# Linear attention gate and suffix decay sums: from float32 matmuls to stacked and split float32r matmuls

## The chip, the cores and the metric

The kernel runs on one core of a Trainium2 chip. The metric is the device time of one execution in microseconds (us). Three runs of the kernel before took 1291.74, 1292.12 and 1295.21 us (median 1292.12). One further execution was recorded by the hardware profiler, and all durations below come from it.

## The reference

One layer of a hybrid encoder is computed for a prompt of 512 tokens and for 8 samples of 16 tokens each (640 rows in all): three token mixers in parallel (stick-breaking attention, a pooling mixer, gated linear attention), cross attention, and a SwiGLU network. The change touches only the decay gates of the linear attention:

```python
log_a = log_sigmoid(lr @ w_gla_a2 + b_gla_a) / 16          # lr: rows x 16, w_gla_a2: 16 x 384
def step(S, inp):                                          # one chunk: 64 prompt rows, or 16 sample rows
    qc, kc, vc, ac = inp
    b = cumsum(ac, axis=1)
    o_inter = einsum('blhk,bhkv->blhv', qc * exp(b), S)
    decay = exp(where(causal, b[:, :, None] - b[:, None, :], -inf))
    att = einsum('bthk,bshk,btshk->bhts', qc, kc, decay)
    o_intra = einsum('bhts,bshv->bthv', att, vc)
    S_new = exp(b[:, -1])[..., None] * S + einsum('bshk,bshv->bhkv', kc * exp(b[:, -1:] - b), vc)
    return S_new, o_inter + o_intra
```

The kernel treats the prompt in four tiles of 128 rows and the eight samples as a fifth tile. The sum `b[:, -1:] - b` is a suffix sum of the gates; it is what `pd` holds below.

## The kernel before, in words

Weights and activations of the large products are held as two float32r parts, a high part (`wh_`, `hT_h`, ...) and the remainder (`wl_`, `hT_l`, ...), and each product is three matmuls (line 114). Small products, those of the linear attention among them, are plain float32 matmuls, which the trace shows as two instructions each.

Instructions of one engine run in program order. That order isn't the order of the source: a scheduler puts the instructions of all engines in order when the program is built, by its own costs and by which buffers come free. Only a few later stages fix their order by hand.

Linear attention runs tile by tile in the order 0, 1, sample, 2, 3. `gla_prep(i)` makes the gates of a tile: transposes of q and k, then `tp_lr` (L653, TensorE) and the copy `lrT` (L656, ScalarE), the gate product `z` (L658; in the rows `z_g`), three ScalarE steps and one VectorE step that give `la` (L660 to L663), the prefix sums `pb` (L667), their copy `bT` and exponential `E`, the suffix sums `pd` (L674) and their exponential. `gla_main(i)` then goes through the levels 64, 32, 16, 8, 4, 2, 1 (the sample tile through the last four): each level makes a tile `X` from `bT` (two subtractions on VectorE, L713 and L714; one, L709, at level 1), an exponential on ScalarE (L715 or L710), multiplies it by k and q (L716, L717), and has four small products `pl` (L721) whose result is copied into `attT` under a mask (L724). The products of a level are told apart by the partitions of `pl`: 64, 96, 112, 120, 124, 126, 127 for level 64 down to level 1. `X` has two buffers. The tile `la` has one buffer, which it shares with `sq` (L782) of `gla_main`.

While this goes on, TensorE also has the projections `ps_n` (the last 190 of them between the first gate and the first level), and after them the gate and branch products `ps_g` and `ps_b` of the branches a and b, which depend on nothing of the linear attention. ScalarE and VectorE turn `ps_g` into a sigmoid (`sgm`, L816 to L819) and multiply `ps_b` by it (`mrg`), and they also split the next weights (`wh_`, L83; `wl_`, L89). Branch c needs the linear attention's output (`tp_oc`).

In the first 50 us VectorE and GpSimd build masks; the gate weights `a2` (in the trace `a`) are loaded by two transfers from GpSimd's queue. `hist` is loaded from SyncE's queue and transposed by TensorE (`tp_h`) just before the products `ps_u`.

Of the kernel before, what the change touches and what calls it, by code (L numbers as in the profile page):

```python
# [8 lines left out]
F32 = mybir.dt.float32  # L9
F32R = mybir.dt.float32r  # L10
# [3 lines left out]
ALU = mybir.AluOpType  # L14
AX = mybir.AxisListType

P = 128
# [9 lines left out]
GW = 384  # L27
# [6 lines left out]
def tile_hybrid_stream_step(  # L34
# [9 lines left out]
    nc = tc.nc  # L44
    PSUM = bass.MemoryType.PSUM

    def open_pool(name, side="left", bufs=1, **kw):
        return tc.alloc_tile_pool(name=name, bufs=bufs, side=side, reuse_waits="tile", **kw)

    const = open_pool("const")  # L50
# [12 lines left out]
    def bank(shape, tag="z", name="ps"):  # L63
        bufs = {"g": 2, "t": 2, "z": 2, "o": 2}[tag]
        return psum.tile(shape, F32, tag=tag, bufs=bufs, name=name)
# [75 lines left out]
    def split(h, l, src):  # L141

        nc.scalar.copy(h, src)  # L143
        nc.vector.tensor_tensor(l, src, h.bitcast(F32), ALU.subtract)  # L144
# [66 lines left out]
    ident = const.tile([P, P], F32, name="ident")  # L211
# [71 lines left out]
    suf = const.tile([P, P], F32, name="suf")  # L283
# [10 lines left out]
    suf_s = const.tile([P, P], F32, name="suf_s")  # L294
# [14 lines left out]
    for hh in (64, 32, 16, 8, 4, 2, 1):  # L309
# [3 lines left out]
        sel(v, [[2 * hh, nb]], hh - 1, -1)  # L313
        lmask[hh] = v
        o += nb
    a2 = const.tile([17, GW], F32, name="a2")
    nc.gpsimd.dma_start(a2[0:16, :], w_gla_a2[0])
    nc.gpsimd.dma_start(a2[16:17, :], b_gla_a[0:1, :])
    gn = const.tile([P, GW], F32, name="gn")
    nc.gpsimd.dma_start(gn, gla_norm[0:1, :].broadcast_to([P, GW]))  # L320
    psc = const.tile([P, 2], F32, name="psc")
# [6 lines left out]
    lr_nat = natc.tile([P, NT, 16], F32, name="lr_nat")  # L328
# [47 lines left out]
    for f in range(2):  # L376
        tp = bank([P, P], "t", "tp_h")
# [51 lines left out]
    for t_i in range(2):  # L429
        un = poolw.tile([P, 256], F32, tag="un", bufs=2, name="un")  # L430
        tp = bank([P, 256], "t", "tp_u")
# [25 lines left out]
    for i in range(NT):  # L457
        tp = bank([P, SBW], "t", "tp_k")
# [176 lines left out]
    glw = open_pool("glw", "right")  # L635
    S = None

    def gla_prep(i):

        sample = i == 4  # L640
        qT = glw.tile([96, 4, P], F32, tag="qT", bufs=2, name="qT")
        kT = glw.tile([96, 4, P], F32, tag="kT", bufs=2, name="kT")
        tp = bank([96, 4, P], "t", "tp_q")
        for h in range(4):
            nc.tensor.transpose(tp[:, h, :], qk_nat[:, i, h * 96:(h + 1) * 96], ident)
        nc.scalar.mul(qT, tp, 96 ** -0.5)
        tp = bank([96, 4, P], "t", "tp_k")
        for h in range(4):
            nc.tensor.transpose(tp[:, h, :], qk_nat[:, i, GW + h * 96:GW + (h + 1) * 96], ident)
        nc.scalar.copy(kT, tp)  # L650

        tp = bank([16, P], "t", "tp_lr")
        nc.tensor.transpose(tp, lr_nat[:, i, :], ident)  # L653
        lrT = glw.tile([17, P], F32, tag="lrT", name="lrT")
        nc.gpsimd.memset(lrT, 1.0)
        nc.scalar.copy(lrT[0:16, :], tp)  # L656
        z = bank([P, GW], "t", "z_g")
        nc.tensor.matmul(z, lrT, a2, start=True, stop=True)  # L658
        la = glw.tile([P, GW], F32, tag="la", name="la")
        nc.scalar.activation(la, z, AF.Abs)  # L660
        nc.scalar.activation(la, la, AF.Exp, scale=-1.0)
        nc.scalar.activation(la, la, AF.Ln, bias=1.0)
        nc.vector.scalar_tensor_tensor(la, z, 0.0, la, ALU.min, ALU.subtract)  # L663

        pb = bank([96, 4, P], "t", "pb")
        for h in range(4):
            nc.tensor.matmul(pb[:, h, :], la[:, h * 96:(h + 1) * 96], tri_s if sample else tri,  # L667
                             start=True, stop=True)
        bT = glw.tile([96, 4, P], F32, tag="bT", bufs=2, name="bT")
        nc.scalar.copy(bT, pb)  # L670
        E = glw.tile([96, 4, P], F32, tag="E", bufs=2, name="E")
        nc.scalar.activation(E, pb, AF.Exp, scale=1.0 / TAU)
        pd = bank([P, GW], "t", "pd")
        nc.tensor.matmul(pd, suf_s if sample else suf, la, start=True, stop=True)  # L674
        kd = qk_nat[:, i, 0:GW]
        nc.scalar.activation(kd, pd, AF.Exp, scale=1.0 / TAU)
        nc.vector.tensor_tensor(kd, kd, qk_nat[:, i, GW:2 * GW], ALU.mult)
        eL = glw.tile([96, 4, NB], F32, tag="eL", bufs=2, name="eL")
        if sample:
            nc.gpsimd.tensor_copy(eL, E.rearrange("p h (b t) -> p h b t", t=16)[:, :, :, 15])  # L680
        else:
            nc.gpsimd.tensor_copy(eL[:, :, 0:1], E[:, :, 127:128])
        nc.vector.tensor_tensor(E, E, qT, ALU.mult)
        return qT, kT, bT, E, eL
# [105 lines left out]

    order = (0, 1, 4, 2, 3)
    pre = gla_prep(0)
    for c in range(5, 7):
        proj_nat(c)
    for j, i in enumerate(order):
        nxt = gla_prep(order[j + 1]) if j + 1 < NT else None
        if i == 4:
            gla_main(i, pre, None)
        else:
            S = gla_main(i, pre, S)  # L800
        pre = nxt
# [34 lines left out]
    for i in range(NT):  # L836
        tp = bank([P, 3, P], "t", "tp_oc")
# [15 lines left out]
    X = resid.tile([P, NT, D], F32, name="X")  # L853
# [687 lines left out]
```

## Time and profile before

| | us |
|---|---|
| median of three runs | 1292.12 |
| profiled execution, its own time | 1288.61 |
| span from first to last instruction | 1286.9 |
| TensorE busy | 1266.3 (98%) |
| VectorE busy | 781.4 (61%) |
| ScalarE busy | 593.2 (46%) |

TensorE's share of the chain that ended last is 93%. An engine's busy time in a stretch of 40 us, subtracted from 40, is its idle time there. "Chain" below is the view of the work that ended last in a stretch, merged into pieces with start, length and count.

### The profile page before, as it was taken

To read this page: it belongs to the slowest core of one execution; us is meant where nothing else is said; L and a number is where in the kernel's file an instruction comes from. 1 tells how busy PE (TensorE), PEld (TensorE's weight loads), DVE (VectorE), ACT (ScalarE), POOL (GpSimd) and SP (SyncE) were. 2 spreads that over 40 slices of the span, in tenths; PEclk is the share of its full clock that TensorE was granted. 3 is DMA by queue.
4 is the path that set the end of the run, shared out by engine and by line. 5 is a ranking of instruction groups with operands and counts; after the bars stand their busy time and mean duration, and the time that the engine had idled before them with its cause. 6 is when DMAs were issued, how large, how long until landed. Compare 5 with 4: busy or idle time off the path is not lost.

```text
span 1286.9 us, 21366 instructions
## 1 busy us (share of the span) xinstructions
PE 1266.3 (98%) x8493; PEld 1154.1 (90%) x8493; DVE 781.4 (61%) x1465; ACT 593.2 (46%) x1191; POOL 41.3 (3%) x162
## 2 busy tenths in 40 slices
PE   8999999999999999999999999999999999999997
PEld 8998777998999999987998888889898989899996
DVE  7343876387478455537535544598466767675667
ACT  5324665455353444535444443475352525243353
POOL 2101111001000000000000000000000000000000
PEclk9999999999999999999999999999999999999999
DMA  7324332101321232232348960243132313132233
GB/s 241 100 80 118 96 102 70 47 16 56 83 65 46 83 93 75 95 131 66 118 161 301 324 228 1 82 148 94 54 107 73 99 51 113 52 99 83 83 107 123
DMA packets 132890, 133.89 MB, mean 104 GB/s; under 512 B 15798, under 2 KB 116741, under 8 KB 132789
## 3 DMA queue, kind: packets, MB, share of 16 engines
q1 hardware_dynamic: 132501, 132.23, 32.8%
q8 instruction: 67, 1.10, 0.4%
q14 instruction: 34, 0.28, 0.1%
q0 software_dynamic: 288, 0.29, 0.1%
HBM read 121.72 MB, written 10.77 MB: 103 GB/s over the span
## 4 chain that ended last, share of the span: by engine, by line
PE 93%; DVE 3%; ACT 2%; DMA 1%; issue 1%; SPq 0%; POOL 0%; DVEq 0%; ACTq 0%
PE ps_g L114 13%; PE fX L1292 11%; PE ps_d L114 8%; PE ps_n L114 7%; PE fZ L1292 5%; PE ps_xq L114 4%; PE ps_b L114 4%; PE acc L1364 4%; PE acc L1363 4%; PE acc L1365 4%; PE ps_qk L114 3%; PE fY L1292 3%; PE pl L721 2%; PE ps_xv L114 2%; PE ps_xk L114 2%; PE z L508 1%
## 5 line engine op out<-in xcount | busy, mean ns | idle before, releaser
L1363 PE MATMUL acc<-wh_o,ga_h 128*128 128x512 f32 (+1 forms) x224 | 87.3, 390 | 0.0
L1364 PE MATMUL acc<-wl_o,ga_h 128*128 128x512 f32 (+1 forms) x224 | 87.2, 389 | 0.0
L1365 PE MATMUL acc<-wh_o,ga_l 128*128 128x512 f32 (+1 forms) x224 | 87.2, 389 | 0.0
L816 ACT ACTIVATE sgm<-ps_g 128x320 f32<-128x320 f32 x48 | 20.9, 436 | 65.9 <-PE ps_g L114 65.8
L1365 PEld LDWEIGHTS acc<-wh_o,ga_l 128*128 128x128 f32 x224 | 42.0, 188 | 9.6
L1363 PEld LDWEIGHTS acc<-wh_o,ga_h 128*128 128x128 f32 x224 | 42.0, 188 | 9.3
L1364 PEld LDWEIGHTS acc<-wl_o,ga_h 128*128 128x128 f32 x224 | 42.1, 188 | 9.2
L1292 PE MATMUL fX<-fT_h,wl_f 128*128 128x320 f32 x160 | 49.5, 309 | 0.0
L1292 PE MATMUL fX<-fT_l,wh_f 128*128 128x320 f32 x160 | 49.4, 309 | 0.0
L1292 PE MATMUL fX<-fT_h,wh_f 128*128 128x320 f32 x160 | 49.4, 309 | 0.0
L1292 PE MATMUL fZ<-S_h,wl_f 128*128 128x320 f32 x160 | 49.4, 309 | 0.0
L1292 PE MATMUL fX<-S_h,wh_f 128*128 128x320 f32 x160 | 49.4, 309 | 0.0
L1292 PE MATMUL fZ<-S_l,wh_f 128*128 128x320 f32 x160 | 49.4, 309 | 0.0
L1292 PE MATMUL fX<-S_l,wh_f 128*128 128x320 f32 x160 | 49.4, 309 | 0.0
L1292 PE MATMUL fZ<-S_h,wh_f 128*128 128x320 f32 x160 | 49.4, 308 | 0.0
L1292 PE MATMUL fX<-S_h,wl_f 128*128 128x320 f32 x160 | 49.3, 308 | 0.0
L143 ACT CAST wh_f<-ra 128x1024 fp32r<-128x1024 f32 x20 | 21.0, 1051 | 45.7 <-PE acc L1365 26.8
L144 DVE TENSOR_TENSOR wl_f<-ta,wh_f 128x1024 fp32r<-128x1024 f32 x20 | 24.5, 1226 | 27.1 <-ACT wh_f L143 27.1
L817 DVE TENSOR_SCALAR sgm<-sgm 128x320 f32<-128x320 f32 x48 | 15.5, 325 | 40.4 <-ACT sgm L816 40.3
L143 ACT CAST wh_f<-ta 128x1024 fp32r<-128x1024 f32 x20 | 21.0, 1049 | 38.7 <-PE acc L1365 29.2
L144 DVE TENSOR_TENSOR wl_f<-ra,wh_f 128x1024 fp32r<-128x1024 f32 x20 | 24.4, 1222 | 22.9 <-ACT wh_f L143 22.7
L1448 DVE TENSOR_TENSOR X<-acc,X 128x512 f32<-128x512 f32 x40 | 27.2, 690 | 17.9 <-PE acc L1365 17.9
(1001 smaller groups left out, 4230.5 us busy)
## 6 DMA issues: line engine op xcount, KB each, us to landing
raw_o<-in_w_ffn_out_dram SPq DMA_DIRECT2D x22, 512.0 KB, 3.5
ra<-in_w_ffn_in_dram SPq DMA_DIRECT2D x40, 256.0 KB, 3.3
rb<-in_w_ffn_in_dram SPq DMA_DIRECT2D x40, 256.0 KB, 3.4
kc<-in_cache_mem_k_dram SPq DMA_DIRECT2D x16, 512.0 KB, 4.8
vc<-in_cache_mem_v_dram SPq DMA_DIRECT2D x16, 512.0 KB, 5.7
raw_mix<-in_w_mix_out_dram SPq DMA_DIRECT2D x8, 512.0 KB, 4.1
raw_xo<-in_w_xo_dram SPq DMA_DIRECT2D x8, 512.0 KB, 4.8
kn<-in_cache_sb_k_dram SPq DMA_DIRECT2D x24, 128.0 KB, 2.5
```

Of the source, the lines that this page charges most:

```text
L114: ins = nc.tensor.matmul(ps, a, b, start=(j == 0), stop=(j == len(todo) - 1))
L143: nc.scalar.copy(h, src)
L144: nc.vector.tensor_tensor(l, src, h.bitcast(F32), ALU.subtract)
L508: nc.tensor.matmul(z[:, j * n:(j + 1) * n], qkT[r, p_, i * P:(i + 1) * P], qkT[r, 3 + p_, 0:n], start=True, stop=True)
L721: nc.tensor.matmul(pl[0:nk, h], X[:, h, 0:nk], mv_, start=True, stop=True)
L816: nc.scalar.activation(s, ps, AF.Exp, scale=-1.0)
L817: nc.vector.tensor_scalar(s, s, 2.0 ** 63, None, ALU.min)
L1292: nc.tensor.matmul(ps, w_, m_, start=(start and j == 0), stop=(stop and j == 11), skip_group_check=True)
L1363: nc.tensor.matmul(ps, ah, wh[:, 0, c0:c0 + w], start=first, stop=False)
L1364: nc.tensor.matmul(ps, ah, wl[:, 0, c0:c0 + w], start=False, stop=False)
L1365: nc.tensor.matmul(ps, al, wh[:, 0, c0:c0 + w], start=False, stop=last)
L1448: nc.vector.tensor_tensor(dst, ps, dst, addop)
```

## The change

The gate product becomes one float32r matmul over 81 rows. The 16 columns of `lr` are split into a high and a low part and laid into columns 0 to 15 (high), 32 to 47 (low) and 64 to 79 (high) of a tile `lr3`, whose columns 16 and 80 hold ones for the bias; `a2` holds the high part of the weights in rows 0 to 16 and 32 to 47 and the low part in rows 64 to 80. The transposed tile is cast to float32r when it is copied. The suffix sums `pd` become two float32r matmuls, of the high and the low part of `la`, with the 0/1 matrix cast to float32r. The low part `la_l` takes one of the two buffers of `X`. The prefix sums `pb` stay float32.

```diff
-    a2 = const.tile([17, GW], F32, name="a2")
-    nc.gpsimd.dma_start(a2[0:16, :], w_gla_a2[0])
-    nc.gpsimd.dma_start(a2[16:17, :], b_gla_a[0:1, :])
+    a2 = const.tile([81, GW], F32R, name="a2")
+    nc.gpsimd.memset(a2.bitcast(F32), 0.0)
+    a2w = open_pool("a2w", "right")
+    a2n = a2w.tile([81, GW], F32, name="a2n")
+    for r_ in (0, 32, 64):
+        nc.gpsimd.dma_start(a2n[r_:r_ + 16, :], w_gla_a2[0])
+    for r_ in (16, 80):
+        nc.gpsimd.dma_start(a2n[r_:r_ + 1, :], b_gla_a[0:1, :])
+    a2h = a2w.tile([81, GW], F32R, name="a2h")
+    nc.vector.tensor_copy(a2[0:17, :], a2n[0:17, :])
+    nc.vector.tensor_copy(a2[32:48, :], a2n[32:48, :])
+    nc.vector.tensor_copy(a2h[64:81, :], a2n[64:81, :])
+    nc.vector.tensor_tensor(a2[64:81, :], a2n[64:81, :], a2h[64:81, :].bitcast(F32), ALU.subtract)
+    a2w.release()
+    suf_r = const.tile([P, 2, P], F32R, name="suf_r")
+    nc.vector.tensor_copy(suf_r[:, 0], suf)
+    nc.vector.tensor_copy(suf_r[:, 1], suf_s)
...
-        tp = bank([16, P], "t", "tp_lr")
-        nc.tensor.transpose(tp, lr_nat[:, i, :], ident)
-        lrT = glw.tile([17, P], F32, tag="lrT", name="lrT")
-        nc.gpsimd.memset(lrT, 1.0)
-        nc.scalar.copy(lrT[0:16, :], tp)
+        lr3 = glw.tile([P, 81], F32, tag="lr3", name="lr3")
+        lrh = glw.tile([P, 16], F32R, tag="lrh", name="lrh")
+        nc.gpsimd.memset(lr3, 0.0)
+        nc.gpsimd.memset(lr3[:, 16:17], 1.0)
+        nc.gpsimd.memset(lr3[:, 80:81], 1.0)
+        nc.scalar.copy(lrh, lr_nat[:, i, :])
+        nc.scalar.copy(lr3[:, 0:16], lrh.bitcast(F32))
+        nc.scalar.copy(lr3[:, 64:80], lrh.bitcast(F32))
+        nc.vector.tensor_tensor(lr3[:, 32:48], lr_nat[:, i, :], lrh.bitcast(F32), ALU.subtract)
+        tp = bank([81, P], "t", "tp_lr")
+        nc.tensor.transpose(tp, lr3, ident)
+        lrT = glw.tile([81, P], F32R, tag="lrT", name="lrT")
+        nc.scalar.copy(lrT, tp)
...
-        nc.tensor.matmul(pd, suf_s if sample else suf, la, start=True, stop=True)
+        la_h = glw.tile([P, GW], F32R, tag="la_h", name="la_h")
+        la_l = glw.tile([P, GW], F32R, tag="X", bufs=2, name="la_l")
+        split(la_h, la_l, la)
+        sr = suf_r[:, 1 if sample else 0]
+        nc.tensor.matmul(pd, sr, la_h, start=True, stop=False)
+        nc.tensor.matmul(pd, sr, la_l, start=False, stop=True)
```

The scheduler puts the stage of the linear attention in another order. On VectorE, this is what stands before in the first tile's levels, from the first write of `attT` (L698) on; the subtractions for level 64 and 32 were already made during the projections, far above, and the second tile's `la` stands between two subtractions of level 8:

```order
L698 TENSOR_TENSOR attT<-pa,ident 128x512
L713 TENSOR_TENSOR X<-bT 96x16x16
L724 COPY_PREDICATED attT<-lm,pl 64x4x64
L714 TENSOR_TENSOR X<-bT 96x16x16
L724 COPY_PREDICATED attT<-lm,pl 96x8x32
L713 TENSOR_TENSOR X<-bT 96x32x8
L663 SCALAR_TENSOR_TENSOR la<-z_g,la 128x384
```

With the change, at the same place, the second tile's `la` and `la_l` come first, and levels 64 and 32 of the first tile follow them:

```order
L727 TENSOR_TENSOR attT<-pa,ident 128x512
L676 TENSOR_TENSOR lr3_3156<-lr_nat_411,lrh_3157 128x16
L687 SCALAR_TENSOR_TENSOR la_2993<-z_g_2991,la_2993 128x384
L144 TENSOR_TENSOR la_l_3009<-la_2993,la_h_3008 128x384
L742 TENSOR_TENSOR X_3026<-bT_2664 96x4x64
L743 TENSOR_TENSOR X_3026<-bT_2664 96x4x64
L742 TENSOR_TENSOR X_3038<-bT_2664 96x8x32
L743 TENSOR_TENSOR X_3038<-bT_2664 96x8x32
L712 TENSOR_TENSOR E_3005<-E_3005,qT_2964 96x512
```

So all levels of a tile now stand behind the next tile's gate, in one block. On TensorE, in the second tile's last levels, this stands before between level 4 (`pl` of 124 partitions) and level 2 (126):

```order
L721 MATMUL pl<-X 124x64 x4
L114 MATMUL ps_g<-hT_l,wh_ga0b 128x320
L114 MATMUL ps_g<-hT_h,wl_ga0b 128x320
L114 MATMUL ps_g<-hT_h,wh_ga0b 128x320
L114 MATMUL ps_g<-hT_l,wh_ga0b 128x320
L114 MATMUL ps_g<-hT_h,wl_ga0b 128x320
L114 MATMUL ps_b<-oa_h,wh_ba_3847 128x320
L114 MATMUL ps_b<-oa_l,wh_ba_3847 128x320
L114 MATMUL ps_b<-oa_h,wl_ba_3849 128x320
L721 MATMUL pl<-X 126x64 x4
```

With the change, the same levels of the same tile, from level 8 (120) on:

```order
L750 MATMUL pl<-X 120x64 x4
L114 MATMUL ps_b<-oa_h,wh_ba_3929 128x320
L114 MATMUL ps_b<-oa_l,wh_ba_3929 128x320
L114 MATMUL ps_b<-oa_h,wl_ba_3931 128x320
L750 MATMUL pl<-X 124x64 x4
L750 MATMUL pl<-X 126x64 x4
L678 MATMUL tp_lr<-ident,lr_3341 81x128
L114 MATMUL ps_g<-hT_h,wh_ga1a 128x320
L114 MATMUL ps_g<-hT_l,wh_ga1a 128x320
L682 MATMUL z_g<-a_379,lrT 128x384
```

Eight large matmuls stood between level 4 and level 2; now there are none, three stand between level 8 and level 4, and two between `tp_lr` and `z_g`.

## Rows read from the trace of the kernel before

**Rows 1.** The page: span, the engines' totals, and TensorE's granted clock by slices.

```profile
span 1286.9 us, 21366 instructions
PE 1266.3 (98%) x8493; PEld 1154.1 (90%) x8493; DVE 781.4 (61%) x1465; ACT 593.2 (46%) x1191; POOL 41.3 (3%) x162
...
PEclk9999999999999999999999999999999999999999
```

**Rows 2.** Busy time by engine, summed over six stretches of 40 us, 200 to 440.

```profile
sum 240.00, PE 235.14 PEld 216.28 DVE 154.56 ACT 116.46 POOL 11.88; mean PE 39.19 PEld 36.05 DVE 25.76 ACT 19.41 POOL 1.98
```

**Rows 3.** Waits of TensorE, 215 to 425 us, the two longest: total, times, longest.

```profile
PE pl L721 <- DVE X L717: 2.6, 4, 1.5
PE ps_b L114 <- ACT sgm L816: 1.1, 2, 0.5
```

**Rows 4.** Chain of work, 215 to 425 us: start, length, piece.

```profile
223.98 0.88 PE z_g L658 x2
...
228.98 24.48 PE ps_n L114 x190
...
256.52 0.84 PE z_g L658 x2
260.17 0.87 PE pb L667 x8
261.04 0.65 PE pd L674 x2
...
342.50 3.50 PE ps_g L114 x24
```

**Rows 5.** Timeline of the first tile's gate: start, length, instruction.

```profile
222.93 0.09 PEld L653 LDWEIGHTS tp_lr<-ident,lr_nat 128*16 128x16 f32 x1
222.93 0.28 PE L653 MATMUL tp_lr<-ident,lr_nat 128*16 128x128 f32 x1
...
223.65 0.25 ACT L656 COPY lrT<-tp_lr 16x128 f32<-16x128 f32 x1
...
224.90 0.49 ACT L660 ACTIVATE la<-z_g 128x384 f32<-128x384 f32 x1 [1.00 <-PE z_g L658]
...
226.61 0.56 DVE L663 SCALAR_TENSOR_TENSOR la<-z_g,la 128x384 f32<-128x384 f32 x1 [3.73 <-ACT la L662]
```

**Rows 6.** Timeline of the last tile, between level 32 and level 16.

```profile
398.56 0.44 DVE L724 COPY_PREDICATED attT<-lm,pl 96x256 f32<-96x256 uint32 x1 [0.75 <-PE pl L721]
...
400.17 0.41 DVE L717 TENSOR_TENSOR X<-X,qT 96x256 f32<-96x256 f32 x1
...
400.73 0.97 PE L721 MATMUL pl<-X 96*112 96x64 f32 x8 [1.52 <-DVE X L717]
```

**Rows 7.** Timeline of the first tile, VectorE, level 8's copy to level 4's last product.

```profile
264.22 0.43 DVE L724 COPY_PREDICATED attT<-lm,pl 120x256 f32<-120x256 uint32 x1
264.55 0.41 DVE L714 TENSOR_TENSOR X<-bT 96x256 f32<-96x256 f32 x1
...
266.16 0.42 DVE L717 TENSOR_TENSOR X<-X,qT 96x256 f32<-96x256 f32 x1
```

**Rows 8.** Timeline of the first 50 us: transfers of `a`, `hist`, its transpose, VectorE's idle time.

```profile
4.40 0.65 POOL L317 DMA_DIRECT2D a<-in_w_gla_a_dram  x1
...
28.47 0.43 SPq L375 DMA_DIRECT2D hist<-in_state_pool_dram  x1
...
30.00 0.74 POOL L217 TENSOR_SCALAR_AFFINE_SELECT seg<-seg 128x128 f32<-128x128 f32 x2
...
43.46 1.23 DVE L89 TENSOR_TENSOR wl_ua<-raw_ua,wh_ua 128x1024 fp32r<-128x1024 f32 x1 [11.45 <-ACT wh_ua L83]
...
46.77 0.37 PE L378 MATMUL tp_h<-ident,hist 120*128 120x120 f32 x2
```

**Rows 9.** Tiles `a` and `hist`: time from issue to landing.

```profile
DMA to landing us min/median/max: 4.8/4.9/5.0
...
DMA to landing us min/median/max: 3.3/3.3/3.3
```

## The prediction, made before the changed kernel ran

> **What bounds the kernel now.** I read the page first: TensorE is busy 1266.3 of 1286.9 us, at full granted clock in every slice [rows 1]. So time is won only where TensorE has less to do, and lost only where it waits longer. The change works in the linear attention, so I read next the busy time by stretches, from 200 to 440 us: TensorE is busy 235.14 of 240 us, VectorE 154.56, ScalarE 116.46 [rows 2]. The waits of TensorE there [rows 3] show what its 4.9 idle us are: 2.6 us in four waits of `pl` for the last VectorE step of `X`, and 1.1 us in two waits of `ps_b` for ScalarE's reading of `ps_g`. The chain of work [rows 4] gives what a matmul takes of TensorE's time when matmuls follow each other; the timelines [rows 5 to 7] give how long the steps between two matmuls of the linear attention take; the last two groups [rows 8, 9] are for the start of the program. In the order, the linear attention ends among the products of branch b, and only branch c uses it, so a later end of it costs nothing; a TensorE instruction that stands in the queue before its operand is ready does.
>
> **What TensorE has less to do.** The price of a float32r matmul comes from 190 of 278 columns in 24.48 us, 0.129 us each [rows 4], or 0.463 ns a column; 24 of 320 columns in 3.50 us give 0.456. For 384 columns that is 0.18 us.
>
> - Gate product: two instructions of 0.84 to 0.88 us together [rows 4] become one of 0.18: 0.66 us less, five tiles, 3.3 us. If the part that lies above `pd`'s 0.65 us for the same columns stays, only 0.47 us go, five times 2.35.
> - Suffix sums: 0.65 us [rows 4] become two of 0.18: 0.29 us less, five times 1.45 us.
> - `tp_lr` has 81 weight columns instead of 16. Its load of 0.09 us [rows 5] becomes longer by less than 0.1 us and lies beside the matmul in front; between 0 and 0.4 us in all, and I take 0.15.
>
> Together 4.6 us, between 3.4 and 4.8.
>
> The Trainium skill, "Perfetto Trace Analysis", section "Engine Utilization", lets float32 in its low-high form cost half the rate. By that rule `pd` would take about 0.35 us before, two float32r matmuls would take as long, and the gain would shrink to that of the gate, about 0.9 us in all, and the time to 1296.5. The row of 0.65 us against 0.18 says a factor of 3.6 [rows 4]; the row decides, and the rule gets no chance of its own.
>
> **What is added off TensorE.** Per tile ScalarE gets `lrh` and two copies of 16 columns (about 0.25 us each by the copy `lrT` [rows 5]) and `la_h` (0.49 us by the first step of `la` [rows 5]); VectorE gets the low part of `lr` (under 0.2 us) and `la_l` (0.56 us by `la` [rows 5]); GpSimd three fills instead of one. With 116 and 155 of 240 us busy [rows 2] this load hides, except where a matmul waits for it; those places follow.
>
> At the start, five transfers instead of two leave GpSimd's queue, and after `seg` at 30.7 us instead of at 4.4. At 0.65 us each and 5.0 us to land [rows 8, 9] they are there by about 39 us, four VectorE steps end by 41, in a gap in which VectorE waited 11.45 us until 43.46 [rows 8]. On SyncE's queue `hist` now stands behind one more store of `va`, and perhaps behind those steps; issued by 41 us and landing 3.3 us later [rows 9], it is there at 44 to 45, and its transpose starts at 46.77 [rows 8]. I cost the start at nothing; if the cover is gone, `tp_h` waits some 1 to 2 us.
>
> **What TensorE waits longer.** `la_l` takes one of the two buffers of `X`, and the order shows what follows: all levels of a tile stand behind the next tile's gate, and TensorE's filler between the levels is thinner. VectorE's steps between two levels can be counted with durations of before. The check is the longest wait of before: from the mask copy at 398.56 to the end of X*q at 400.58, then `pl` at 400.73, of which TensorE stood idle 1.52 us [rows 6]; its filler was just too short for five VectorE steps. A VectorE step of 256 columns holds the queue 0.33 us [rows 7].
>
> - First tile, level 8 to 4: VectorE's list (mask copy, three subtractions, one short step, two products) is the one of before, which took from 264.22 to 266.58, 2.4 us [rows 7]. TensorE now has ten matmuls there, 1.5 us: 0.9 us wait. Level 1 has three steps after level 2's end, about 1.4 us, against two matmuls, `tp_lr` and the gate product, 0.6: 0.8 us.
> - Second tile, level 8 to 4: four steps, 1.4 us, against three matmuls, 0.45: 1.0 us. Level 2 comes directly after level 4, and between them VectorE has two short steps, a weight remainder of 1.23 us (the size of `wl_ua` [rows 8]), a mask copy and two products, 2.8 us against the 0.8 us of level 4's own matmuls: 2.0 us.
> - Fourth tile in order (prompt tile 2), level 8 to 4: again 1.4 against 0.45: 1.0 us. Last tile and sample tile: filler of ten or more, 0.5 us together.
> - Suffix sums: `la_h` (0.49) and `la_l` (0.56) end about 1.2 us after `la`, while `pb` and the first half of `pd` cover 0.87 and 0.18 [rows 4]: 0.2 us, in five tiles 1.0.
> - Gate product: in three tiles it stands two matmuls (0.3 us) behind `tp_lr`; transposition, cast and hand-over take about 0.6 us: 0.9 us in all.
>
> That is 8.1 us. The 1.1 us of `ps_b` I leave as they are [rows 3], which makes 9.2. Of before's waits, the reordering ends the 2.6 us of `pl` and keeps the 1.1; with small gaps of 0.2 they were 3.9. So the waits grow by 5.3 us. Their bounds: 1 us less than before (a new order can also remove waits without adding any), or 10 more (the 1.52 us of [rows 6] at two levels of each of five tiles, 15.2, less the 3.9, rounded down for the short sample tile).
>
> **Sum.** 5.3 less 4.6 is 0.7 us more: 1288.61 becomes 1289.3 for the profiled execution. The runs' median lies 3.5 us above the profiled execution's own time, so 1292.8 us is predicted. This is no change: a difference below 0.3%, 3.9 us, can't be told from none in measurements of this kernel, whose three runs span 3.5 us.
>
> **Rivals.**
>
> 1. *Only the matmuls count.* TensorE waits as much as before, in other places, and the gain of 4.6 stands: 1287.5. For it: the scheduler keeps independent `ps_g` and `ps_b` at hand, and before it left only 3.9 us of waits in 240. Against it: before, levels 64 and 32 of the first tile were made long ahead, and the order of the change shows levels with three matmuls or none between them.
> 2. *One buffer of `X` less decides.* Level 32 needs the buffer of `la_l` and can't be written until the second half of `pd` has read it. VectorE, in order, stops there, and behind it queue E*q, the masks and the steps on `sgm` and `mrg`, on which `ps_b` waits. If each of the four tiles with a following gate loses, beyond the waits counted, the 1.52 us of [rows 6] once, that is 6 us: 1299. Half of it, 3.2 us more than my sum, is where slower than before begins to be seen. For it: VectorE's share before was 155 of 240, and higher among the levels. Against it: `pb` and `pd` come right after `la`, so the buffer is held for little more than 2 us.
> 3. *The product doesn't get cheaper.* If the 81-row product keeps a gap like the one above `pd`'s length, the gain is 3.6 instead of 4.6: 1293.8, no change either. Small, and inside the likeliest case.
>
> **Numbers.** No change, from 1289.5 to 1295.5 by its own terms (waits 2 to 8 more): 0.55, rival 3 within it. Faster: 0.25, all of rival 1 with waits that grow by less than 0.7 us. Slower: 0.20, of which rival 2 has most and a late `hist` little. The range that leaves out 0.2 goes from 1287.0 (rival 1 and the lower bound's half) to 1298.0 (most of rival 2).
>
> **What would show it.** One instruction per tile of about 0.18 us in the chain for the gate product and two for `pd` prove the gain; a piece of 0.65 or 0.84 there disproves it. The waits of TensorE between 215 and 425 us should come to 8 to 10 us, most of them `pl` for X*q, the longest in the second tile between level 4 and level 2, and some 2 us of `pd` and `z_g` for `la_l` and `lrT`. Under 5 us in all, my count of VectorE's steps is wrong and the kernel is faster; over 12 us, rival 2 holds. Idle time of TensorE before 60 us and after 440 us should be as it was; a wait of `tp_h` would show that the start isn't covered.

## The result, and the profile after

The changed kernel takes 1314.03 us (median of 6 runs, 1310.99 to 1317.79), the kernel before 1292.48 beside it (6 runs, 1290.33 to 1295.21): a ratio of 1.017 [1.0155, 1.0185]. It is slower by 21.5 us. The prediction of 1292.8, no change, was wrong; its range ended at 1298.0. The profiled execution took 1313.41 us, of which the span is 1311.7.

The page of the changed kernel, the lines of [rows 1]:

```profile
span 1311.7 us, 21417 instructions
PE 1285.9 (98%) x8488; PEld 1175.7 (90%) x8488; DVE 788.0 (60%) x1481; ACT 597.6 (46%) x1211; POOL 41.4 (3%) x176
...
PEclk9999999987997899999999999999999999999999
```

TensorE has less to multiply, and yet is busy 19.6 us longer. The last line says why: in slices 9, 10, 13 and 14 the granted clock isn't full. Busy time by stretches (columns: stretch, its length, busy time of PE, PEld, DVE, ACT and POOL, granted clock, share and rate of the DMAs) shows it in numbers; the sum answers to [rows 2]:

```profile
200.00:240.00 40.00, 39.07 (x311) 34.17 (x311) 20.04 (x43) 22.55 (x58) 3.47 (x13) 1.00 0.15 42
240.00:280.00 40.00, 38.30 (x276) 36.46 (x276) 21.71 (x53) 19.88 (x45) 1.20 (x8) 0.95 0.17 50
280.00:320.00 40.00, 37.53 (x228) 35.97 (x227) 28.73 (x74) 19.86 (x44) 0.94 (x5) 0.76 0.13 37
...
400.00:440.00 40.00, 37.39 (x231) 36.07 (x232) 28.80 (x83) 16.20 (x32) 0.83 (x2) 0.79 0.00 1
sum 240.00, PE 231.09 PEld 214.76 DVE 144.68 ACT 113.50 POOL 10.16; mean PE 38.52 PEld 35.79 DVE 24.11 ACT 18.92 POOL 1.69
```

TensorE is idle 8.9 of the 240 us, where it was idle 4.9. That growth, 4.0 us, is a little less than the 5.3 that the prediction had counted, and small beside 21.5 us. From 280 to 320 us it is busy 37.53 us, but at 0.76 of its clock. In pieces of 2 us (stretch, length, busy time of TensorE, granted clock, DMAs) the same place reads:

```profile
296.00:298.00 2.00, 1.99 (x15) 1.00 0.00 0
298.00:300.00 2.00, 0.90 (x7) 0.89 0.00 0
300.00:302.00 2.00, 0.71 (x4) 0.50 0.12 13
302.00:304.00 2.00, 2.00 (x10) 0.50 0.82 249
...
314.00:316.00 2.00, 2.00 (x10) 0.50 0.00 0
316.00:318.00 2.00, 2.00 (x14) 0.84 0.03 8
318.00:320.00 2.00, 2.00 (x18) 1.00 0.00 0
```

The clock is at the lower of its two levels, 1.2 GHz, from about 299.6 to 316.6 us; TensorE runs ten instructions in 2 us where at 2.4 GHz it ran 15 to 18. It stood idle once just ahead of the fall, and once more when the clock was already low (start, length, instruction, idle time before it and what ended it):

```profile
299.10 1.46 PE L750 MATMUL pl<-X 96*124 96x64 f32 x8 [1.11 <-ACT wh_ga2a L83]
301.86 1.94 PE L750 MATMUL pl<-X 96*126 96x64 f32 x8 [1.29 <-DVE X L746]
```

These are level 4 and level 2 of the second tile, the place where the prediction had its longest wait. Three more such stretches begin at about 275.7, 408.8 and 443 us: the first behind four waits of 0.2 to 0.5 us (270 to 276), the second behind a wait of 0.5 us and inside one of 1.1, the third behind three of 0.3, 0.8 and 0.4. In the kernel before, waits as long had passed at full clock: two in the same tile, and in the last tile the wait of [rows 6], which is longer than any in this stage of the changed kernel (2 us pieces as above):

```profile
282.00:284.00 2.00, 1.42 (x11) 1.00 0.00 0
288.00:290.00 2.00, 1.47 (x12) 1.00 0.00 0
398.00:400.00 2.00, 1.20 (x12) 1.00 0.00 0
400.00:402.00 2.00, 1.26 (x10) 1.00 0.00 0
```

So a short wait stands at each of the four falls, but a wait of this length doesn't always bring one.

Summed over pieces of 10 us from 200 to 480 us, ten times one less the granted clock is 23.9 us. With 5.2 us more idle time there and 3.5 us less work (below) this gives 25.6 us; the span grew by 24.8. About 1.5 us of the waits lie inside low stretches and so are counted twice, by half. The waits of TensorE, 215 to 425 us, beside [rows 3] (total, times, longest):

```profile
PE pl L750 <- DVE X L746: 2.6, 3, 1.3
PE ps_b L114 <- ACT sgm L845: 1.9, 4, 0.5
PE pl L750 <- ACT wh_ga2a L83: 1.1, 1, 1.1
PE ps_g L114 <- DVE mrg L853: 0.5, 1, 0.5
PE tp_lr L678 <- ACT kT L666: 0.3, 1, 0.3
```

### The profile page after: what moved, and what is told of

The parts are those of the page before. It is cut to its first block, busy times and chain, and to the rows that moved or that the text cites. A ratio compares the mean times of both kernels' runs of the same rounds, so it can differ in the third digit from the quotient of the medians.

```text
span 1311.7 us, 21417 instructions
## 1 busy us (share of the span) xinstructions
PE 1285.9 (98%) x8488; PEld 1175.7 (90%) x8488; DVE 788.0 (60%) x1481; ACT 597.6 (46%) x1211; POOL 41.4 (3%) x176
## 4 chain that ended last, share of the span: by engine, by line
PE 91%; DVE 4%; ACT 2%; DMA 1%; issue 1%; POOL 0%; SPq 0%; DVEq 0%; ACTq 0%
PE ps_g L114 13%; PE fX L1321 11%; PE ps_d L114 8%; PE ps_n L114 7%; PE fZ L1321 5%; PE ps_xq L114 4%; PE ps_b L114 4%; PE acc L1392 4%; PE acc L1393 4%; PE acc L1394 4%; PE ps_qk L114 3%; PE fY L1321 3%; PE pl L750 2%; PE ps_xv L114 2%; PE ps_xk L114 2%; PE z L524 1%
## 5 line engine op out<-in xcount | busy, mean ns | idle before, releaser
L750 PEld LDWEIGHTS pl<-X 96*120 96x120 f32 (+6 forms) x256 | 33.9, 208 | 7.7 <-issue 4.8
L750 PE MATMUL pl<-X 96*120 96x64 f32 (+6 forms) x256 | 35.2, 289 | 5.0 <-DVE X L746 3.7
```

Of the source, the lines that this page charges most:

```text
L750: nc.tensor.matmul(pl[0:nk, h], X[:, h, 0:nk], mv_, start=True, stop=True)
```

## Experiments

First theory: the new order leaves TensorE with several short waits close together, and its granted clock falls to 1.2 GHz behind them; the arithmetic itself gains. Second theory: the lighter products, or the new start of the gate, cost the clock wherever `la_l` lies. A table of all runs in which the linear attention was changed stands first. "Idle" and "clock" are read from 28 pieces of 10 us of the profiled execution, 200 to 480 us: the idle time of TensorE, and the sum of ten times one less the granted clock.

| kernel | median us | ratio to before | idle | clock |
|---|---|---|---|---|
| before | 1291.1 to 1292.5 | 1 | 4.9 | 0.0 |
| changed kernel | 1314.03 | 1.0170 [1.0155, 1.0185] | 10.1 | 23.9 |
| e5_hold | 1311.25 | 1.0152 [1.0134, 1.0171] | 9.4 | 18.8 |
| e3_pd | 1310.03 | 1.0141 [1.0127, 1.0155] | 10.0 | 13.6 |
| e2_gate | 1298.62 | 1.0054 [1.0040, 1.0069] | 7.5 | 12.0 |
| e1_own | 1299.95 | 1.0060 [1.0047, 1.0073] | 8.8 | 13.7 |
| g_rep3 | 1288.92 | 0.9979 [0.9968, 0.9990] | 4.8 | 3.4 |
| e1_rep3 | 1303.60 | 1.0070 [1.0045, 1.0096] | 8.1 | 17.0 |
| g_x3 | 1306.44 | 1.0106 [1.0088, 1.0124] | 10.4 | 15.3 |
| j2_after | 1293.02 | 1.0010 [1.0000, 1.0021] | 3.5 | 0.0 |
| k1_after128 | 1298.76 | 1.0048 [1.0032, 1.0064] | 5.9 | 5.1 |
| k2_after42 | 1298.31 | 1.0049 [1.0033, 1.0065] | 6.1 | 5.1 |
| k3_own128 | 1298.95 | 1.0051 [1.0034, 1.0068] | 5.6 | 11.9 |
| k4_own42 | 1298.09 | 1.0046 [1.0030, 1.0062] | 5.4 | 8.5 |

**Holding the buffer, no arithmetic (e5_hold).** In the kernel before:

```diff
-        nc.tensor.matmul(pd, suf_s if sample else suf, la, start=True, stop=True)
+        la_x = glw.tile([P, GW], F32, tag="X", bufs=2, name="la_x")
+        nc.vector.tensor_copy(la_x, la)
+        nc.tensor.matmul(pd, suf_s if sample else suf, la_x, start=True, stop=True)
```

> The kernel before, with one edit: the gate's logarithm is copied once more on VectorE into a buffer of X, and the decay sums read the copy, in float32 as before. No product of TensorE changes; only the buffer is held and the order follows. Theory 1: the clock falls to 1.2 GHz in stretches between 270 and 450 us, and the time is 1308 to 1320 us, though TensorE has exactly the work of the kernel before. Theory 2: full clock, 1291 to 1298 us.

Measured 1311.25 us against 1291.55: with TensorE's work of before, 19.7 us are lost. Two of its stretches (columns as in the 2 us pieces above):

```profile
270.00:280.00 10.00, 8.36 (x44) 0.75 0.01 2
...
410.00:420.00 10.00, 10.00 (x49) 0.57 0.01 2
```

So most of the loss doesn't need the new products. It comes with the held buffer and the order that it brings.

**The two halves, and the whole without the buffer (e3_pd, e2_gate, e1_own).** e3_pd is the kernel before with the two-part `pd`; e2_gate has the 81-row gate product alone; e1_own is the changed kernel with

```diff
-        la_l = glw.tile([P, GW], F32R, tag="X", bufs=2, name="la_l")
+        la_l = glw.tile([P, GW], F32R, tag="st", bufs=1, name="la_l")
```

> The decay sums alone in two parts, with la_l in a buffer of X; the gate product stays one product of float32. Theory 1: the order of TensorE is that of the changed kernel, so the clock falls in two or more stretches between 270 and 450 us, 1304 to 1317 us. Theory 2 in the form that the gate product is at fault: full clock, 1290 to 1295 us.

> The gate product alone (81 rows, new start); the decay sums pd stay one product of float32, and no buffer of X is taken. Theory 1: full clock, about 1287 to 1293 us (five products of 0.84 us become about 0.2 each, a few tenths of new waits). Theory 2: the clock falls at least in part, over 1298 us.

> The whole change, except that the low part of the decay (la_l) is written to the place that the sample tile's state (tag st) uses much later, not to one of the two buffers of X. The arithmetic is that of the changed kernel; the order of TensorE goes back to nearly that of the kernel before (levels 64 and 32 of a tile stand among the next tile's gate again). Theory 1 (the buffer of X packs the levels together, TensorE idles in 2 us stretches, and its granted clock falls to 1.2 GHz behind them): granted clock 1.00 in every window from 240 to 480 us, 1286 to 1292 us. Theory 2 (the lighter products or the new start cost the clock, wherever la_l lies): clock falls between 270 and 450 us as in the changed kernel, about 1308 to 1316 us.

e3_pd came as the first theory said (1310.03). The other two did not: the gate alone costs 7.1 us and the whole change outside of `X` 8.4, each with the clock low between 287 and 307 us and from 409 on. This was a point for the second theory, though only e2_gate lies where that had it (over 1298); e1_own lies between the two ranges. The timeline of e2_gate shows five waits ahead of its first fall, at about 293 us:

```profile
286.58 0.41 PE L114 MATMUL ps_b<-oa_h,wh_ba 128*128 128x320 f32 x1 [0.53 <-ACT sgm L837]
...
288.45 1.93 PE L742 MATMUL pl<-X 96*124 96x64 f32 x16 [0.28 <-DVE X L738]
290.70 0.34 PE L675 MATMUL tp_lr<-ident,lr 128*81 128x128 f32 x1 [0.32 <-ACT kT L663]
291.39 0.45 PE L679 MATMUL z_g<-a,lrT 81*128 81x384 f32 x1 [0.35 <-ACT lrT L677]
292.27 1.43 PE L742 MATMUL pl<-X 96*127 96x64 f32 x8 [0.43 <-DVE X L738]
```

The scheduler counts what a product costs. A cheaper gate product alone gives another order and other waits, so the product's weight and the order had to be told apart.

**The gate product three times (g_rep3, e1_rep3).** e2_gate, and e1_own, with

```diff
-        nc.tensor.matmul(z, lrT, a2, start=True, stop=True)
+        for _ in range(3):
+            nc.tensor.matmul(z, lrT, a2, start=True, stop=True)
```

> The gate product alone, as in e2_gate, but the product of 81 rows is issued three times into the same place (each starts the sum anew, so the result is the same). TensorE gets two needless products of about 0.18 us per tile, 1.8 us in all, and the scheduler, which counts them, puts the levels of a tile back almost where they stood in the kernel before. The new start of the gate (lr3, its copies, the wider transpose) stays. Theory 1 (order and waits decide the clock): granted clock 1.00 from 240 to 480 us and 1288 to 1292 us, so faster than e2_gate by 6 us or more with more work on TensorE. Theory 2 (the new start or the lighter product itself costs the clock): falls as in e2_gate, 1298 to 1302 us.

> The whole change with la_l in the place of the sample tile's state (e1_own) and the gate product issued three times. Arithmetic gain left on TensorE against the kernel before: about 1.5 us of the gate, 1.4 of the decay sums. Theory 1: if the order leaves waits of TensorE no closer together than before, full clock and 1287 to 1291 us; the packed levels of the second and the third tile in this order could still bring one fall, then 1292 to 1297. Theory 2: 1299 to 1303 us.

g_rep3 does about 1.7 us more work than e2_gate (in the first tile 0.63 us from start to next start for three products, 0.29 for one; in the second 0.52 and 0.18) and is 9.7 us faster; it is faster than the kernel before by 0.21% [0.10, 0.32] and the best of all that ran. The new start of the gate is in it, so this start costs nothing. One short fall is left in its trace:

```profile
400.00:410.00 10.00, 9.61 (x52) 0.66 0.09 26
```

e1_rep3 missed both ranges of the first theory; 1303.60 lies just above that of the second. Its order isn't that of before (in the second tile `pb` and `pd` stand ahead of level 32). The clock is low from 310 to 317 us, behind waits of 0.4 to 0.6 us, and from 392 to 419, behind one of 1.5 us of `pl` for X*q; its longest wait, 1.9 us of `ps_g` for `mrg`, lies inside that stretch. So more work than in e1_own didn't help here; j2_after, next, puts work closer to the gaps.

**Needless work where TensorE waits (j2_after).** The changed kernel, ahead of the products of a level:

```diff
+            if hh in (8, 4, 2, 1):
+                jv = qT.rearrange("p h t -> p (h t)")[:, 0:256]
+                pj = pl.rearrange("p h n c -> p (h n c)")
+                nc.tensor.matmul(pj[0:nk], kT[:, 0, 0:nk], jv, start=True, stop=True)
```

> The changed kernel with one needless float32 product of 256 columns (k by q, about 0.43 us) in front of the products of each of the levels 8, 4, 2 and 1, 20 in all, some 8.6 us of work more on TensorE, which doesn't wait for X and so stands in the idle time. Theory 1: TensorE idles less ahead of the levels, the clock falls in fewer or shorter stretches, and the time is 1298 to 1312 us although work is added. Theory 2 (the falls don't come from the waits): 1318 to 1324 us with the falls of the changed kernel.

Measured 1293.02: 21 us less than the changed kernel and below the first theory's range, though each of the 20 products took up to 0.48 us of TensorE's time, 9.6 us in all at most. The clock is full from 200 to 480 us, and the waits of TensorE, 215 to 455 us, are short:

```profile
PE po_g L777 <- DMA st<-in_state_gla_dram: 0.8, 1, 0.8
PE pl L755 <- DVE X L746: 0.4, 1, 0.4
PE pa L726 <- DVE attT L758: 0.3, 1, 0.3
```

The second theory had 1318 to 1324 and falls here; the lighter products and the new start are all in this kernel, at full clock. TensorE is busy 1273.2 us, 6.9 more than in [rows 1] and so less than was added: the arithmetic of the change does gain. Without the 9.6 us the kernel would stand at 1283.4 at the least, an estimate; part of that work fills time in which TensorE would otherwise wait. Two things changed together here: the needless products also moved others (between level 4 and level 2 of the second tile stand seven `ps_g`, where the changed kernel has none), and they put products of 256 columns among those of 64. So this run clears the lighter products, but doesn't tell whether the waits or the run of small products lowered the clock.

**Half the needless work (k1 to k4).** k1_after128: 128 columns instead of 256. k2_after42: 256 columns, at the levels 4 and 2 only. k3_own128 and k4_own42: the same two on e1_own.

> As j2_after, with needless products of 128 columns instead of 256: about 4.8 us of added work (half of the 0.48 us that one took of TensorE's time) instead of 9.6. If the waits are what lowers the clock, half the work may still cover enough of them: 1287 to 1293 us at full clock; where a stretch of waits is left uncovered, one fall and 1293 to 1300. If the added work counts and not what it covers, 1298 to 1304.

> The changed kernel with one needless product of 256 columns in front of the levels 4 and 2 only, ten in all, 4.8 us. The waits ahead of level 8 and level 1 and those of ps_b stay. If the waits that lower the clock are those of the levels 4 and 2: full clock, 1287 to 1292 us. If the other waits suffice for a fall: 1293 to 1305.

> The whole change with la_l outside of X (e1_own) and needless products of 128 columns at the levels 8, 4, 2 and 1, 4.8 us. Full clock would give about 1286 to 1291 us (8 to 12 less than e1_own); a fall left gives 1293 to 1298.

> The whole change with la_l outside of X and one needless product of 256 columns at the levels 4 and 2, 4.8 us. Full clock 1286 to 1291 us; a fall left gives 1293 to 1298.

All four take 1298 to 1299 us, slower than before by half a per cent, and falls remain (5 to 12 us by the table). k1 and k2 lie in the range with a fall left, k1 also in that where added work counts; k3 and k4 lie just above theirs. Beside the changed kernel k1 and k2 still win 15 us with about 5 us of added work; beside e1_own k3 and k4 win only 1.0 and 1.9.

**Three buffers of X (g_x3).** e2_gate with `bufs=3` at every tile with the tag `X`.

> The gate product alone, as in e2_gate, with three buffers of X instead of two. A level's X can then be made while two others wait for TensorE; the order packs the last levels of a tile (4, 2, 1) directly behind each other. If it is the hold of X's buffers that makes TensorE wait, the waits of pl for X shrink and the clock stays full: 1286 to 1291 us. If it is the thin filler between the levels, wherever X lies, the clock falls at least twice: 1296 to 1306 us.

1306.44 us, 7.8 more than with two buffers: the second tile's last three levels stand directly behind each other, and `pl` waits 6.6 us for X*q, 2.0 at the longest. A buffer more doesn't help here; that levels without products between them do the harm fits, but buffers and order changed together.

**Late, in the same order (x1_late12, x2_late3).** In all of these the order and the waits changed together. The feed-forward stage is ordered by hand, so there TensorE can be made to wait in the kernel before with every one of its instructions in its old place:

```diff
-            split(h, l, src)
+            split(h, l, src); [nc.vector.tensor_copy(l, l) for _ in range(3 if self.n in (12, 13) else 0)]
```

(x1_late12: 12 copies, of the part `t4` of unit 12 alone.)

> The kernel before; in one unit of the feed-forward stage (unit 12, between about 1040 and 1130 us), VectorE copies a weight remainder of 512 columns onto itself 12 times before TensorE may use it, some 4 to 8 us late. TensorE's instructions and their order are those of the kernel before, one by one. Theory 1 (a stretch of waits is followed by 1.2 GHz, whatever the order): TensorE waits some 1 to 6 us there, the granted clock falls to half behind it for about 6 to 16 us, and the loss is the wait plus 3 to 8 us. Theory 3 (the order of the products decides): the clock stays 1.00 and the loss is the wait alone. If the slack hides the delay, nothing is told.

> As x1_late12, but the remainders of all four parts of units 12 and 13 are copied three times each: several shorter waits in a row in place of one. Theory 1: waits of 3 to 15 us in all, with one or more falls of the clock among them, loss larger than the waits by 3 us or more. Theory 3: full clock, loss equal to the waits.

x2_late3 takes 1298.3 us, 1.0052 [1.0032, 1.0072], some 6 us (4 to 9) more than the 1292.38 beside it. Its trace has one wait of 4.2 us, of `fX` for the remainder, not the several that were meant, and then, in pieces of 1 us:

```profile
1086.00:1087.00 1.00, 0.09 (x1) 0.92 0.00 0
1087.00:1088.00 1.00, 1.00 (x4) 0.50 0.00 0
1088.00:1089.00 1.00, 1.00 (x6) 0.50 0.00 0
1089.00:1090.00 1.00, 1.00 (x5) 0.50 0.07 4
1090.00:1091.00 1.00, 1.00 (x8) 0.88 0.79 115
1091.00:1092.00 1.00, 1.00 (x9) 1.00 0.95 389
```

With TensorE's order unchanged, a wait alone is followed by 1.2 GHz. The pieces lose 1.7 us (0.08, three times 0.5, 0.12), less than the 3 us that the first theory had; wait and clock together are 5.9 us. That this is close to the 6 of the medians is in part luck: the profiled execution was the fastest of five (1295.4), and the clock was also low for some 3.4 us at the program's start. So a wait of 4.2 us was followed by a fall in the old order; that waits of 0.2 to 1.3 us bring it in the same way isn't shown by this run.

x1_late12 was hidden by slack: a wait of 0.3 us, 0.9999 [0.9983, 1.0015]. But its profiled execution, with the linear attention as before, has a fall that the prediction's trace didn't have, and no wait ahead of it:

```profile
257.00:258.00 1.00, 1.00 (x7) 1.00 0.50 83
258.00:259.00 1.00, 1.00 (x10) 0.72 1.02 337
259.00:260.00 1.00, 1.00 (x5) 0.50 0.30 105
260.00:261.00 1.00, 1.00 (x5) 0.50 0.00 0
261.00:262.00 1.00, 1.00 (x7) 0.57 0.00 0
```

Ahead of it, from 253.5 us on, TensorE ran `tp_q`, `tp_k`, `pa`, `tp_lr`, `pl`, `z_g` and a few `ps_g` without a pause. So waits aren't the only thing that goes before a fall: among the linear attention's small float32 products the clock can fall without one, in one execution and not in another of the same instructions. This leaves another reading untested: that the run of small products lowers the clock, and waits among them only add to it. The runs of the kernel before fit falls that come in some executions and not in others: over the 59 recorded beside the experiments the mean granted clock goes from 0.991 to 0.999, and the time rises by about 1.0 us for each 0.001 less (correlation -0.79). Not all of that need be the linear attention: from about 11 to 15 us, at the program's start, the clock was low in four of the sixteen profiled executions (j2_after, k1_after128, k2_after42, x2_late3) and full in the others. What sets a fall off stays open.

## Why the prediction was wrong, step by step

- **The step that failed** stands in its first paragraph: time "lost only where it waits longer". Each wait was priced at its own length. The clock was read as full [rows 1] and left out of the sum, the bounds and all rivals; it cost 23.9 us, and the waits themselves 5.2. What sets the falls off is known only so far: in the changed kernel a short wait among small products stands at each. The 3.5 us between the profiled execution and the median, taken as given, were probably the same clock in part: that execution had a mean of 0.999, and the median of the 59 runs above is 0.997.
- **Less work on TensorE**: right in sign, too large. At full clock (j2_after) the gate product takes 0.28 us, start to next start, in four of five tiles, not 0.18, and `pd` 0.27 and 0.28:

```profile
257.06 0.44 PE L682 MATMUL z_g<-a,lrT 81*128 81x384 f32 x1
257.34 0.31 PE L114 MATMUL ps_g<-hT_l,wh_ga0a 128*128 128x320 f32 x1
...
284.93 0.42 PE L702 MATMUL pd<-la_h,suf_r 128*128 128x384 f32 x1
285.20 0.44 PE L703 MATMUL pd<-la_l,suf_r 128*128 128x384 f32 x1
285.48 0.31 PE L114 MATMUL ps_g<-hT_h,wl_ga0b 128*128 128x320 f32 x1
```

  Beside the 0.84 and 0.65 of [rows 4] that is 0.56 and 0.10 us, in five tiles 2.8 and 0.5; where the second half of `pd` follows more quickly, 0.2 and 1.0. The gain is 3.3 to 3.8 us, not 4.6. Rival 3 had the size (3.6), half by luck: it put the whole shortfall on the gate product, and as much or more of it was `pd`'s. The price by columns was taken from long rows of equal products; alone among others most cost 0.1 us more.
- **The start**: right. No wait of `tp_h` shows before 60 us, and g_rep3, which has the new start, is faster than before.
- **The waits**: near in sum (7.3 us idle from 215 to 425, where 8 to 10 were foreseen), so that by its own sign the prediction would have stood; and the second tile's levels 4 and 2 were among the longest (1.11 and 1.29, against 1.0 and 2.0), with level 4 of the fourth tile (1.11, against 1.0). The parts fit less well: the first tile's two waits, 1.7 us by the sum, came to 0.2, and the two hand-overs, `pd` and `z_g`, 1.9 by the sum, show no wait worth a row; `ps_b` grew instead, from 1.1 to 1.9. From 440 to 480 us, where idle time should have stayed as it was, it went from 0.0 to 1.2.
- **Rival 2**, one buffer of `X` less: e5_hold shows that the held buffer alone brings most of the loss. VectorE's stop until `pd` has read the buffer is small in the changed kernel and larger in e5_hold (waits of VectorE, 215 to 425 us, first the changed kernel, then e5_hold):

```profile
DVE X L742 <- PE pd L703: 0.3, 1, 0.3
...
DVE X L715 <- PE pd L676: 2.2, 2, 1.3
```

  So the stop doesn't explain the 21.5 us, and g_x3 shows that a buffer more doesn't help. The price of 6 us was again a price of waits.
- **Rival 1**, only the matmuls count: no run shows its gain of 4.6. g_rep3, in nearly the order of before, is 0.21% faster, and j2_after, where the clock is full, pays for its gain with the needless work.

As a sum, clock and idle time less the work saved explain the spans of the changed kernel, e5_hold, e2_gate and g_rep3 within 1 us, of e1_own and e3_pd within 2.5. Not every difference between executions is in that sum: the profiled one of x1_late12 is 5.3 us longer than that of [rows 1], and its fall and its wait give 2.0. The Trainium skill, "TensorE: Matmul & The Clock Gate", section "HAM oscillation — how this bites in real kernels", tells of a clock that falls in one long gap between products and costs half of the time that it stays low. The second part agrees here (in x2_late3 products of 320 columns follow each other every 0.27 us while the clock reads 0.50 and every 0.15 at full clock, and the sum of 23.9 us goes by such halves); of the first, x2_late3 is a case, with its 4.2 us, but in this stage of the changed kernel no wait was longer than 1.3 us, and ahead of the fall in x1_late12 there was none.

## What to carry to other kernels

Where TensorE sets the time, a wait costs its length and, if it stands among small products, perhaps a fall of the clock that costs several times as much; so read the granted clock of every run before pricing a change, and take a spread in it as a sign of an edge. Read it in short pieces: a page's digit of 9 stands for 90% or more, and j2_after shows 9 in every slice although its clock was low for 3.4 us at the start. A product made cheaper also changes the order that a scheduler builds by its cost: compare the idle time around it, not the product alone. Needless products in the gaps are a quick test of whether the change's own work is the price.

## What was not expected of the hardware

- The clock stayed at 1.2 GHz for 17 us behind a wait of 1.11 us, with one of 1.29 inside and TensorE busy all along after it (2.00 of 2.00 us from 302 on), among the products of the linear attention; behind a wait of 4.2 us it came back within 4 us, among the dense products of the feed-forward stage. What ends a low stretch wasn't tried.
- It fell once with no wait ahead (x1_late12), and it stayed full through a wait of 1.52 us in the kernel before [rows 6].
- Three equal products of 384 columns in a row took 0.63 us in the first tile (g_rep3), one alone 0.29 at the same place (e2_gate): the second and the third added 0.17 each.
